# Two of the three top-16 decodes of the last routing pair, cut into steps and put beside the first expert blocks

## The chip, the cores and the metric

The kernel runs on one core of a Trainium2 chip. The metric is the device time of one execution in microseconds (us); lower is better. The time of the kernel before is the median of 3 runs.

## What is computed

One layer of a bidirectional encoder over 1024 tokens of width 1024, in 8 tiles of 128 tokens: an input projection, two kinds of attention, an output projection, a LayerNorm, and then a product-key expert layer (PEER), which is where the change lies:

```python
def peer(x, w_q, sub_keys, u, v):
    ...
    q = (xf @ w_q).reshape(n, PEER_HEADS, 2, PEER_QDIM // 2)
    sc = jnp.einsum('nhpc,hpkc->nhpk', q, sub_keys).astype(jnp.float32)
    s_top, i_top = lax.top_k(sc, PEER_TOPK)
    cand = (s_top[:, :, 0, :, None] + s_top[:, :, 1, None, :]).reshape(n, PEER_HEADS, PEER_TOPK * PEER_TOPK)
    ...
    fs, fpos = lax.top_k(cand, PEER_TOPK)
    eidx = jnp.take_along_axis(cand_idx, fpos, axis=-1)
    g = jax.nn.softmax(fs, axis=-1)
    ...
        h = jnp.einsum('cd,chkd->chk', xc, u[ec])
        a = (jax.nn.gelu(h.astype(jnp.float32), approximate=False) * gc).astype(xc.dtype)
        return jnp.einsum('chk,chkd->cd', a, v[ec])
```

For each token and each of 8 heads, two lists of 16 best keys of 128 are formed, their best 16 sums are picked (16 of 16,384 experts), and the token's output is the gated sum over its 128 experts. The layer ends in a second LayerNorm.

## The kernel before

The first 1107 us do projection, attention and routing, two tiles at a time; `route(pr)` treats tiles 2pr and 2pr+1. Per tile, routing makes 16 lists of the best 16 keys (`top16`: tiles `stop` for the values, `itop` for the indices), and `decode` (L176 to L235) turns these into 128 expert indices `eidx` and 128 gates: candidate sums `cv`, a second `top16` over them for each head, and then two sweeps of 16 small products into `big`, each closed by two reductions over `big` (L206, L221), all on VectorE (DVE), with one Exp on ScalarE (ACT).

The experts are then applied in two ways. Tiles 0 to 4 ("dense", ND = 5) go through all 16,384 experts in 128 blocks of 128 (`hstage`, `vres`, `vflush`, called from the loop at L771): per block two weight tiles of 512 KB are loaded, split into a high and a low part (ACT makes `uh`, `vh`; DVE makes `ul`, `vl`, both L86 and L87), the matmuls `h` follow (L91 to L93, 48 of 320 columns), Gelu on ACT, a product with the gates `gt` on DVE, and 30 matmuls of 512 columns for the output (`po`, `fl`). Their gates come from dense tables: those of tiles 0 and 1 are scattered into `gs` by 256 indirect DMAs of GpSimd (POOL, L165), those of tiles 2 to 4 are built in SBUF (`build`, L582) and written to `gd`. Tiles 5 to 7 ("gathered") take their 128 experts one by one: POOL gathers one row of `uv` (u and v beside each other) per token (L656, 1 MB each, four buffers), DVE makes the dot product with the token (L658), ACT its Gelu, DVE the product with the gate (L663) and adds the scaled v row to `acc` (L668; the first of a tile is L666). These are 3 x 128 = 384 gathers; `gather_gen` yields after each, and the block loop asks for as many as its line 778 says, about three a block.

The order of the work on each engine is not the order of the code. A scheduler that estimates times lays out each engine's queue when the kernel is built, from the data dependences, the room in the pools and the order of the code as priority. On the chip each engine then takes its own queue strictly in that order.

The decode's temporary tiles lie in the pool `rs`, on the right side of SBUF. When routing ends (`late.close()`, L628), the gather's pools (`x1p`, `gp`, `ga`) take that room, so that what goes there waits for the last instruction that used `rs`. The LayerNorm constants `lnt` (2 x 1024 numbers per partition) are loaded once for the first LayerNorm and again by `load_ln(1)` (L637) for the second, which first happens for tile 5, late in the expert blocks.

Of the kernel before, what the change touches and what calls it, by code (L numbers as in the profile page):

```python
# [11 lines left out]
F32 = mybir.dt.float32  # L12
# [9 lines left out]
P = 128  # L22
# [35 lines left out]
def trunk(ctx, tc, x, xt, wqk, wo, gn, sink, biasa, biasb, ln, wq, keyst, uv, ut, vt, out):  # L58
# [114 lines left out]
            new.append(st.ins)  # L173
        added[t, h] = new

    def decode(idx, g, sv, iv, pool, t=None):  # L176
        s2 = sv.rearrange("p (h two) k -> p h two k", two=2)
        fi = pool.tile([P, 8, 2, TOPK], F32, name="fi", bufs=1)
        nc.vector.tensor_copy(fi, iv.rearrange("p (h two) k -> p h two k", two=2))
# [8 lines left out]
        pos = pool.tile([P, 8, TOPK], U32, name="pos", bufs=1)  # L188
        for h in range(8):
            top16(fs[:, h, :], pos[:, h, :], cv[:, h, :], pool, NCAND)  # L190
        pf = pool.tile([P, 8, TOPK], F32, name="pf", bufs=1)
        nc.vector.tensor_copy(pf, pos)
        dlt = pool.tile([P, 8, TOPK - 1], F32, name="dlt", bufs=1)
# [8 lines left out]
        for a in range(1, TOPK):  # L202
            nc.vector.scalar_tensor_tensor(big[:, a % 8, :, :], pf, START[a] - 0.5,
                                           dlt[:, :, a - 1:a].to_broadcast([P, 8, TOPK]), op0=OP.is_ge, op1=OP.mult)
            if a % 8 == 7:
                nc.vector.tensor_reduce(ef if a == 7 else e2, bsum, AX.X, OP.add)  # L206
        nc.vector.tensor_add(ef, ef, e2)
# [8 lines left out]
        for b in range(TOPK):  # L216
            nc.vector.scalar_tensor_tensor(big[:, b % 8, :, :], pf, float(b),
                                           fi[:, :, 1, b:b + 1].to_broadcast([P, 8, TOPK]),
                                           op0=OP.is_equal, op1=OP.mult)
            if b % 8 == 7:  # L220
                nc.vector.tensor_reduce(ef if b == 7 else e2, bsum, AX.X, OP.add)  # L221
        nc.vector.tensor_add(ef, ef, e2)
# [11 lines left out]
        nc.vector.reciprocal(gs, gs)  # L234
        nc.vector.tensor_mul(gv, gv, gs[:, :, None].to_broadcast([P, 8, TOPK]))  # L235


    late = ExitStack()

    with ExitStack() as att:  # L240
# [278 lines left out]
        def route(pr):  # L519
# [14 lines left out]
                    nc.scalar.dma_start(xd[1, :, :, t * P:(t + 1) * P], f(tl[:, :, tok]))  # L534
            stop_ = {t: rs.tile([P, 16, TOPK], F32, name="stop", bufs=4) for t in tiles}
            itop = {t: rs.tile([P, 16, TOPK], U32, name="itop", bufs=4) for t in tiles}
            for c in range(16):
                if pr == 0 and c % 4 == 0:
                    raw = r1.tile([P, P, GC], F32, name="stage").rearrange("p a c -> p (a c)")
                    raw = raw.rearrange("p (n k c) -> p n k c", n=4, k=KT)  # L540
                    nc.sync.dma_start(raw, wq[c:c + 4].rearrange("n p k c -> p n (k c)"))
                kt = rw.tile([P, P], F32, name="kt")
                nc.sync.dma_start(kt, keyst[:, c, :])
                hi = rw.tile([P, KT, P], F32R, name="qhi")
                lo = rw.tile([P, KT, P], F32R, name="qlo")
                if pr == 0:
                    split(hi, lo, raw[:, c % 4])
                    nc.gpsimd.dma_start(wqd[c, 0], f(hi))
                    nc.gpsimd.dma_start(wqd[c, 1], f(lo))
                else:  # L550
                    nc.sync.dma_start(f(hi), wqd[c, 0])
                    nc.sync.dma_start(f(lo), wqd[c, 1])
                ps = ps_q.tile([P, 4, P], F32, name="pq").rearrange("p a b -> p (a b)")[:, :2 * P]
                for k in range(KT):
                    nc.tensor.matmul(ps, hi[:, k, :], th[:, k, :], start=(k == 0), stop=False)
                    nc.tensor.matmul(ps, hi[:, k, :], tl[:, k, :], start=False, stop=False)
                    nc.tensor.matmul(ps, lo[:, k, :], th[:, k, :], start=False, stop=(k == KT - 1))
                q = rw.tile([P, 2 * P], F32, name="q")
                nc.scalar.copy(q, ps)
                pc = ps_q.tile([P, 4, P], F32, name="pq")  # L560
                for n in range(2):
                    nc.tensor.matmul(pc[:, n, :], q[:, n * P:(n + 1) * P], kt, start=True, stop=True)
                sc = rw.tile([P, 2, P], F32, name="sc")
                nc.scalar.copy(sc, pc[:, 0:2, :])
                for n, t in enumerate(tiles):
                    top16(stop_[t][:, c, :], itop[t][:, c, :], sc[:, n, :], rs, P)
            dense = []
            for t in tiles:
                if t >= ND:
                    decode(eidx[t], gate[t], stop_[t], itop[t], rs)  # L570
                    continue
                idx = rs.tile([P, P], I32, name="idxd", bufs=4)
                g = rs.tile([P, P], F32, name="gated", bufs=4)
                decode(idx, g, stop_[t], itop[t], rs, t if t < NS else None)
                (dense if t < NS else todo).append((t, idx, g))
# [58 lines left out]
    nc.sync.dma_start(f(dl), xd[1])  # L634
    x1p = ctx.enter_context(tc.tile_pool(name="x1p", bufs=2, side="right"))
    x1 = {}
    load_ln(1)  # L637
    gp = ctx.enter_context(tc.tile_pool(name="gp", bufs=GBUF, side="right"))
    ga = ctx.enter_context(tc.tile_pool(name="ga", bufs=1, side="right"))
    sm = ctx.enter_context(tc.tile_pool(name="sm", bufs=2))  # L640
# [37 lines left out]
    def pump(n):  # L678
        while n > 0 and done[0] < total:
            next(gen)  # L680
            done[0] += 1
            n -= 1

    dn = ctx.enter_context(tc.tile_pool(name="dn", bufs=2))
    ph = ctx.enter_context(tc.tile_pool(name="ph", bufs=1, space=PSUM))
    RES = 3
# [84 lines left out]
    for e in range(ne):  # L771
# [3 lines left out]
        if pend is not None:  # L775
            vflush(*pend)
        pend = (e, a)
        while fed < min(total, total * (e + 4) // ne):
            pump(1)
            fed += 1  # L780
    vres(*pend)
# [81 lines left out]
```

## Time and profile before

| | us |
|---|---|
| median of 3 runs (2978.54 to 2978.84) | 2978.63 |
| the profiled execution, device time | 2985.32 |
| its span from first to last instruction | 2981.6 |
| TensorE (PE) busy | 2733.9 |
| DVE busy | 2408.1 |
| ACT busy | 1202.3 |
| POOL busy | 1065.1 |

A row of the timeline gives start, duration, engine, line, operation and operands, and in brackets the idle time of the engine before it and what ended it. A row of the windows view gives for a stretch of time the busy time and the number of instructions of PE, PE's weight loads, DVE, ACT and POOL, then the clock that PE was granted (1.00 is 2.4 GHz, 0.50 is 1.2 GHz), the share of DMA engines busy and GB/s. All times are us from the start of the span. Durations overlap their successor's start by some hundredths of a us, so what an operation costs on a full queue is the distance of two starts.

### The profile page before, as it was taken

How to read it: one execution, taken by the hardware profiler on the slowest of the kernel's cores; microseconds unless marked ns; L12 is line 12 of the kernel's file. 1: busy time of each engine (PE TensorE's matmuls, PEld its weight loads, DVE VectorE, ACT ScalarE, POOL GpSimd, SP SyncE). 2: the span in 40 equal slices, each digit the busy share in tenths (PEclk: the TensorE clock that was granted, in tenths of full speed). 3: DMA queues.
4: the chain of work that ended last, by engine and by line, in shares of the span. 5: the costliest groups of instructions: out<-in, count | busy, mean ns of one | idle time of the engine just before them, and what ended most of it. 6: DMA issues, size and time to landing. Idle time of an engine off the chain costs nothing.

```text
span 2981.6 us, 43327 instructions
## 1 busy us (share of the span) xinstructions
PE 2733.9 (92%) x15569; PEld 2357.3 (79%) x15569; DVE 2408.1 (81%) x5427; ACT 1202.3 (40%) x2486; POOL 1065.1 (36%) x732
## 2 busy tenths in 40 slices
PE   6887899897997867999999999999999999999996
PEld 4776577575785766888998899898888898988885
DVE  2344267887979988898998989999989999998965
ACT  2343154342786762333333343333333333333332
POOL 1111001078888881333333323333333333333300
PEclk8998989898997988999999999999999999999998
DMA  7688598897977767988998989998998898998851
GB/s 233 200 271 269 177 322 296 260 262 180 267 223 221 220 161 265 348 331 324 353 331 332 332 329 335 336 347 334 330 344 327 321 353 322 342 349 332 329 210 46
DMA packets 384886, 854.37 MB, mean 287 GB/s; under 512 B 83616, under 2 KB 243360, under 8 KB 333728
## 3 DMA queue, kind: packets, MB, share of 16 engines
q0 software_dynamic: 124224, 433.43, 41.3%
q1 hardware_dynamic: 230816, 388.82, 38.5%
q10 hardware_dynamic: 29632, 29.37, 3.1%
q8 instruction: 122, 2.00, 0.3%
q14 instruction: 92, 0.75, 0.1%
HBM read 765.21 MB, written 86.11 MB: 286 GB/s over the span
## 4 chain that ended last, share of the span: by engine, by line
PE 48%; DVE 5%; DMA 4%; issue 3%; ACT 2%; POOL 1%; SPq 0%; ACTq 0%; POOLq 0%; DVEq 0%
PE h L91 9%; PE h L92 8%; PE h L93 8%; PE po L736 5%; PE po L737 5%; PE po L738 5%; PE fl L737 3%; PE fl L736 3%; PE fl L738 3%; DMA uv<-in_uv_dram,eidx 2%; DMA raw<-in_ut_dram 2%; DVE uv L658 1%; DVE acc L668 1%; POOL uv L656 1%; DVE vl L87 1%
## 5 line engine op out<-in xcount | busy, mean ns | idle before, releaser
L656 POOL DMA_INDIRECT uv<-in_uv_dram,eidx x384 | 570.4, 1486 | 1162.5 <-DVE acc L668 688.5
L91 PE MATMUL h<-dh,uh 128*128 128x320 f32 x2048 | 641.3, 313 | 49.0 <-ACT uh L86 25.6
L93 PE MATMUL h<-dh,ul 128*128 128x320 f32 x2048 | 634.6, 310 | 0.8 <-DVE ul L87 0.8
L92 PE MATMUL h<-dl,uh 128*128 128x320 f32 x2048 | 634.1, 310 | 0.0
L658 DVE SCALAR_TENSOR_TENSOR uv<-uv,xg 128x1024 f32<-128x1024 f32 x384 | 467.4, 1218 | 43.1 <-DMA uv<-in_uv_dram,eidx 37.3
L165 POOL DMA_INDIRECT gs<-gated,idxd x256 | 434.9, 1699 | 171.3 <-DMA qlo<-wqd 87.0
L668 DVE SCALAR_TENSOR_TENSOR acc<-uv,hh,acc 128x1024 f32<-128x1024 f32 x381 | 487.6, 1280 | 4.3
L91 PEld LDWEIGHTS h<-dh,uh 128*128 128x128 f32 x2048 | 385.7, 188 | 83.7 <-ACT gl L718 48.6
L92 PEld LDWEIGHTS h<-dl,uh 128*128 128x128 f32 x2048 | 385.9, 188 | 10.9
L93 PEld LDWEIGHTS h<-dh,ul 128*128 128x128 f32 x2048 | 385.7, 188 | 4.9 <-DVE ul L87 1.5
L736 PE MATMUL po<-vh,ah 128*128 128x512 f32 x768 | 288.2, 391 | 1.5 <-ACT ah L86 1.5
L737 PE MATMUL po<-vl,ah 128*128 128x512 f32 x768 | 287.8, 391 | 0.0
L662 ACT ACTIVATE hh<-hh 128x1 f32<-128x1 f32 x384 | 77.6, 202 | 476.3 <-DVE uv L658 474.9
L738 PE MATMUL po<-vh,al 128*128 128x512 f32 x768 | 260.8, 391 | 0.0
L764 ACT COPY fl<-fl 128x512 f32<-128x512 f32 x252 | 147.1, 584 | 278.7 <-PE fl L738 278.5
L765 DVE TENSOR_TENSOR facc<-facc,fl 128x512 f32<-128x512 f32 x252 | 172.6, 685 | 72.8 <-ACT fl L764 72.6
L718 ACT ACTIVATE gl<-h 128x320 f32<-128x320 f32 x256 | 111.4, 435 | 254.5 <-PE h L93 244.4
L736 PE MATMUL fl<-vh,ah 128*128 128x512 f32 x512 | 201.8, 394 | 3.0 <-ACT fl L764 3.0
L737 PE MATMUL fl<-vl,ah 128*128 128x512 f32 x512 | 201.9, 394 | 0.0
L738 PE MATMUL fl<-vh,al 128*128 128x512 f32 x512 | 199.6, 390 | 0.0
L87 DVE TENSOR_TENSOR ul<-raw,uh 128x1024 fp32r<-128x1024 f32 x128 | 156.1, 1220 | 52.6 <-ACT uh L86 51.7
L86 ACT CAST uh<-raw 128x1024 fp32r<-128x1024 f32 x128 | 134.2, 1049 | 116.8 <-DMA raw<-in_ut_dram 60.7
(201 smaller groups left out, 5389.2 us busy)
## 6 DMA issues: line engine op xcount, KB each, us to landing
raw<-in_ut_dram SPq DMA_DIRECT2D x128, 512.0 KB
raw<-in_vt_dram SPq DMA_DIRECT2D x128, 512.0 KB
qhi<-wqd SPq DMA_DIRECT2D x48, 512.0 KB
qlo<-wqd SPq DMA_DIRECT2D x48, 512.0 KB
gd<-stage SPq DMA_DIRECT2D x12, 2048.0 KB
gt<-gd SPq DMA_DIRECT2D x32, 768.0 KB
wraw<-in_wqk_dram SPq DMA_DIRECT2D x36, 512.0 KB
bt<-in_biasb_dram SPq DMA_DIRECT2D x64, 288.0 KB
```

Of the source, the lines that this page charges most:

```text
L87: nc.vector.tensor_sub(lo, raw, f(hi))
L91: nc.tensor.matmul(ps, wh, mh, start=first, stop=False)
L92: nc.tensor.matmul(ps, wh, ml, start=False, stop=False)
L93: nc.tensor.matmul(ps, wl, mh, start=False, stop=last)
L165: st = nc.gpsimd.indirect_dma_start(out=gs, out_offset=bass.IndirectOffsetOnAxis(ap=idx[:, k:k + 1], axis=0), in_=g[:, k:k + 1], in_offset ...
L656: nc.gpsimd.indirect_dma_start(out=u, out_offset=None, in_=uv, in_offset=bass.IndirectOffsetOnAxis(ap=eidx[t][:, k:k + 1], axis=0))
L658: nc.vector.scalar_tensor_tensor(u[:, 0:D], u[:, 0:D], 1.0, x1[t], op0=OP.mult, op1=OP.mult, accum_out=hh[:, k:k + 1])
L668: nc.vector.scalar_tensor_tensor(acc, u[:, D:], hh[:, k:k + 1], acc, op0=OP.mult, op1=OP.add)
L736: nc.tensor.matmul(ps, ah[:, cs], vh[:, js], start=first, stop=False)
L737: nc.tensor.matmul(ps, ah[:, cs], vl[:, js], start=False, stop=False)
L738: nc.tensor.matmul(ps, al[:, cs], vh[:, js], start=False, stop=last)
L765: nc.vector.tensor_add(acc[:, j, :], acc[:, j, :], fl)
```

## The change

The decode of tiles 6 and 7, the last two, leaves `route(3)`. `decode` becomes a generator (`decode_steps`) that stops after each head's `top16` and after every fourth product, 16 times per tile; the other tiles run it to its end at once as before. For tiles 6 and 7 the lists `stop` and `itop` are written into the room of `lnt` instead of the pool `rs`, the decode's temporaries lie in the same room and in a new tile `side` (4.5 KB per partition, in the pool `dx` of the expert stage), and the block loop advances the generator two steps per block, 16 blocks in all, after which `load_ln(1)` is called. The pace at which the blocks ask for gathers changes with it: two a block for the first 18 blocks, then about 3.2.

```diff
-    def decode(idx, g, sv, iv, pool, t=None):
+    def decode(*args):
+        for _ in decode_steps(*args):
+            pass
+
+    def decode_steps(idx, g, sv, iv, pool, t=None):
...
             top16(fs[:, h, :], pos[:, h, :], cv[:, h, :], pool, NCAND)
+            yield
...
+            if a % 4 == 3:
+                yield
...
+            if b % 4 == 3:
+                yield
...
+    held = {}
+    lflat = lnt.rearrange("p a d -> p (a d)")
...
+            self.at = dict(fi=(lflat, 1024), fs=(lflat, 1280), pf=(lflat, 1408), dlt=(lflat, 1536), of=(lflat, 1536),
+                           pos=(lflat, 1792), ei=(lflat, 1792), e2=(lflat, 1920), cv=(side, 0), t16=(side, 512),
+                           big=(side, 0), ef=(side, 1024), gs=(side, 0))
...
+            if pr == 3:
+                for n, t in enumerate(tiles):
+                    stop_[t] = carve(lflat, 512 * n, [P, 16, TOPK])
+                    itop[t] = carve(lflat, 512 * n + 256, [P, 16, TOPK], U32)
+                    held[t] = stop_[t], itop[t]
...
             for t in tiles:
+                if t in held:
+                    continue
...
-    load_ln(1)
...
+    side = dx.tile([P, 9 * P], F32, name="side")
+
+    def held_decodes():
+        for t in sorted(held):
+            yield from decode_steps(eidx[t], gate[t], *held[t], Carve(side))
+
+    hd = held_decodes()
...
-        while fed < min(total, total * (e + 4) // ne):
+        for _ in range(2 if hd is not None else 0):
+            if next(hd, 0) == 0:
+                hd = None
+                load_ln(1)
+                break
+        while fed < min(total, 2 * e + 4 if e < 18 else 40 + (total - 40) * (e - 17) // (ne - 21)):
```

What the scheduler made of it, on the two engines on which the expert blocks' first matmuls depend. In these rows `gate_105`, `gate_106` and `gate_107` belong to tiles 5, 6 and 7, `eidx_103` to tile 6, and x2 at the end is a repeat count.

DVE before, from the end of tile 6's decode to the first weight splits of the blocks (the first row with `ul` is block 0's weight split):

```order
L224 TENSOR_TENSOR eidx_103<-ef,of 128x128
L195 SCALAR_TENSOR_TENSOR dlt<-dlt,wrow 128x120
L87 TENSOR_TENSOR ul<-raw,uh 128x1024
L203 SCALAR_TENSOR_TENSOR big<-pf,dlt 128x128 x7
L87 TENSOR_TENSOR vl<-raw,vh 128x1024
L87 TENSOR_TENSOR ul<-raw,uh 128x1024
L206 TENSOR_REDUCE ef<-big 128x128
L87 TENSOR_TENSOR vl<-raw,vh 128x1024
```

DVE now, first where the first gathered row is used, in the middle of tile 6's decode, whose temporaries are `lnt` and `side`:

```order
L239 TENSOR_TENSOR gate_106<-lnt 128x128
L197 CAST lnt<-lnt 128x128
L208 SCALAR_TENSOR_TENSOR side<-lnt 128x128 x7
L213 TENSOR_REDUCE side<-side 128x128
L208 SCALAR_TENSOR_TENSOR side<-lnt 128x128 x8
L695 SCALAR_TENSOR_TENSOR uv,hh<-uv,xg 128x1024
L213 TENSOR_REDUCE lnt<-side 128x128
L700 TENSOR_TENSOR hh<-hh,gate_105 128x1
```

and then, with 78 instructions between that first `uv,hh` row and it, where block 0's `ul` stands:

```order
L187 TENSOR_TENSOR side<-lnt 128x8x16
L705 SCALAR_TENSOR_TENSOR acc<-uv,hh,acc 128x1024
L124 MAX lnt<-side 128x8 x8
L125 MAX_INDEX lnt<-lnt,side 128x8
L126 MATCH_REPLACE side<-lnt,side 128x50
L125 MAX_INDEX lnt<-lnt,side 128x8 x7
L127 MAX lnt<-side 128x8
L128 MAX_INDEX lnt<-lnt,side 128x8
L126 MATCH_REPLACE side<-lnt,side 128x50
L127 MAX lnt<-side 128x8
L128 MAX_INDEX lnt<-lnt,side 128x8
L87 TENSOR_TENSOR ul<-raw,uh 128x1024
```

Before, the first gathered row is used behind the `ul` of block 3; now five `uv,hh` rows, the whole second half of tile 6's decode and the beginning of tile 7's stand ahead of the first `ul`. Tile 7's decode ends (its `eidx`) between the `ul` of blocks 5 and 6.

ACT before, from the last Exp of the decode to the first Gelu of block 0:

```order
L231 ACTIVATE gate_106<-gate_106 128x128
L616 COPY stage<-pr 128x4x128
L231 ACTIVATE gate_107<-gate_107 128x128
L86 CAST uh<-raw 128x1024
L86 CAST vh<-raw 128x1024
L86 CAST uh<-raw 128x1024
L86 CAST vh<-raw 128x1024
L718 ACT_TABLE_LOAD
L718 ACTIVATE gl<-h 128x320
```

ACT now, the same place:

```order
L240 ACTIVATE gate_106<-gate_106 128x128
L699 ACT_TABLE_LOAD
L699 ACTIVATE hh<-hh 128x1 x5
L83 DMA lnt<-in_ln_dram 128x1024
L86 CAST uh<-raw 128x1024
L86 CAST vh<-raw 128x1024
L86 CAST uh<-raw 128x1024
L699 ACTIVATE hh<-hh 128x1
L762 ACTIVATE gl<-h 128x320
```

The Gelus of the first five gathered rows and one load of `lnt` now stand ahead of block 0's `uh`; the Exp of tile 7 stands behind block 0's Gelus, between two table loads.

## Rows read from the trace of the kernel before

**Rows 1.** Busy time by engine, of the whole span.
```profile
PE 2733.9 (92%) x15569; PEld 2357.3 (79%) x15569; DVE 2408.1 (81%) x5427; ACT 1202.3 (40%) x2486; POOL 1065.1 (36%) x732
```

**Rows 2.** Windows: gap ahead of the expert blocks, their start, their long middle.
```profile
1107.70:1133.30 25.60, 0.00 (x0) 0.00 (x0) 22.31 (x116) 2.76 (x6) 7.82 (x5) 0.52 0.83 244
1133.30:1160.00 26.70, 22.84 (x119) 20.82 (x120) 24.94 (x52) 9.25 (x12) 0.90 (x1) 0.88 0.39 129
1160.00:2900.00 1740.00, 1719.56 (x9570) 1549.31 (x9569) 1574.22 (x2292) 622.89 (x1246) 569.53 (x384) 1.00 0.90 332
```

**Rows 3.** Timeline of PE: last matmuls of routing, first of block 0.
```profile
1106.33 1.36 PE L615 MATMUL pr<-pi,qj 128*128 128x128 f32 x8 [0.63 <-ACT qj L611]
1133.34 0.64 PE L91 MATMUL h<-dh,uh 128*128 128x320 f32 x1 [25.65 <-ACT uh L86]
...
1134.60 0.64 PE L93 MATMUL h<-dh,ul 128*128 128x320 f32 x1 [0.36 <-DVE ul L87]
```

**Rows 4.** Timelines of ACT and SP's DMA queue: block 0's weights.
```profile
1132.25 1.04 ACT L86 CAST uh<-raw 128x1024 fp32r<-128x1024 f32 x1 [7.02 <-DMA raw<-in_ut_dram]
...
1119.07 0.37 SPq L700 DMA_DIRECT2D gt<-gs  x1
...
1124.24 2.64 SPq L709 DMA_DIRECT2D raw<-in_ut_dram  x1
```

**Rows 5.** Waits of SP's queue, 1080 to 1200 us (total, times, longest).
```profile
SPq L700 <- DMA gs<-gated,idxd: 9.1, 2, 8.5
```

**Rows 6.** Timeline of POOL: last scatter, first gather.
```profile
1114.59 2.15 POOL L165 DMA_INDIRECT gs<-gated,idxd  x1 [0.30 <-issue]
1159.10 1.02 POOL L656 DMA_INDIRECT uv<-in_uv_dram,eidx  x1 [42.36 <-DVE eidx L224]
```

**Rows 7.** Timeline of DVE: last product of the table build, then the decode.
```profile
1104.73 0.68 DVE L606 TENSOR_TENSOR qj<-iota,tt 128x512 f32<-128x512 f32 x1
...
1110.29 1.85 DVE L206 TENSOR_REDUCE ef<-big 128x128 f32<-128x1024 f32 x1
1112.06 0.19 DVE L234 RECIPROCAL gs<-gs 128x8 f32<-128x8 f32 x1
...
1113.08 0.07 DVE L125 MATCH_VALUE_LOAD pos<-fs,cv 128x8 f32 x1
...
1113.26 0.07 DVE L125 MATCH_VALUE_LOAD pos<-fs,cv 128x8 f32 x1
...
1113.44 1.68 DVE L203 SCALAR_TENSOR_TENSOR big<-pf,dlt 128x128 f32<-128x128 f32 x8
1115.04 0.28 DVE L235 TENSOR_TENSOR gate<-gate,gs 128x128 f32<-128x128 f32 x1
1115.25 0.08 DVE L128 MATCH_VALUE_LOAD pos<-fs,t 128x8 f32 x1
```

**Rows 8.** Timeline of DVE: block 0's split, end of the decode, first gathered rows.
```profile
1133.32 1.23 DVE L87 TENSOR_TENSOR ul<-raw,uh 128x1024 fp32r<-128x1024 f32 x1 [3.31 <-ACT uh L86]
1134.47 1.49 DVE L203 SCALAR_TENSOR_TENSOR big<-pf,dlt 128x128 f32<-128x128 f32 x7
...
1157.95 0.29 DVE L224 TENSOR_TENSOR eidx<-ef,of 128x128 int32<-128x128 f32 x1
1159.60 0.82 DVE L722 TENSOR_TENSOR gl<-gl,gt 128x640 f32<-128x640 f32 x1 [1.36 <-ACT gl L718]
...
1168.13 1.23 DVE L658 SCALAR_TENSOR_TENSOR uv<-uv,xg 128x1024 f32<-128x1024 f32 x1 [5.59 <-issue]
...
1172.78 1.28 DVE L668 SCALAR_TENSOR_TENSOR acc<-uv,hh,acc 128x1024 f32<-128x1024 f32 x1
1173.98 1.22 DVE L658 SCALAR_TENSOR_TENSOR uv<-uv,xg 128x1024 f32<-128x1024 f32 x1
1175.12 0.08 DVE L658 DVE_READ_ACCUMULATOR uv<-uv,xg 128x1 f32 x1
```

**Rows 9.** Timeline of ACT: the table load ahead of the first Gelu.
```profile
1139.08 1.28 ACT L718 ACT_TABLE_LOAD   x1
```

More of the change, by code (lines that the diff above doesn't have):

```diff
@@ L235, in decode, with carve, __init__, tile @@
         nc.vector.tensor_mul(gv, gv, gs[:, :, None].to_broadcast([P, 8, TOPK]))
+    held = {}
+    lflat = lnt.rearrange("p a d -> p (a d)")
+    def carve(flat, at, shape, dt=F32):
+        n = int(np.prod(shape[1:]))
+        ap = flat[:, at:at + n]
+        if dt is not F32:
+            ap = ap.bitcast(dt)
+        names = "abcd"[:len(shape) - 1]
+        return ap.rearrange(f"p ({' '.join(names)}) -> p {' '.join(names)}", **dict(zip(names, shape[1:])))
+    class Carve:
+        def __init__(self, side):
+            self.at = dict(fi=(lflat, 1024), fs=(lflat, 1280), pf=(lflat, 1408), dlt=(lflat, 1536), of=(lflat, 1536),
+                           pos=(lflat, 1792), ei=(lflat, 1792), e2=(lflat, 1920), cv=(side, 0), t16=(side, 512),
+                           big=(side, 0), ef=(side, 1024), gs=(side, 0))
+        def tile(self, shape, dt, name, bufs=1):
+            flat, n = self.at[name]
+            return carve(flat, n, shape, dt)
     late = ExitStack()
```

## The prediction, made before the changed kernel was run

> **What bounds the kernel now.** I read the busy times first: PE is busy for 92% of the span, DVE for 81% [rows 1]. That is an average over unlike stages, so the windows come next. In the long middle of the expert blocks, 1160 to 2900 us, PE is busy 1719.6 of 1740 us at full clock, DVE 1574.2 [rows 2]: there PE is the limit, and the 9570 matmuls of that row take 1740 / 9570 = 0.182 us each, so that a block of 78 (48 for `h`, 30 for the output) takes 14.2 us. What PE loses ahead of the blocks is therefore not won back in them; the place to look at is the passage from routing to the blocks. There PE stands still from 1107.7 to 1133.3 and gets its first `h` only when ACT has made `uh` [rows 3]; ACT waited for the transfer of `raw` [rows 4]; that transfer stands in SP's queue behind the loads of `gt`, which start at 1119.07 [rows 4] because they wait for the last scatters into `gs` to land [rows 5], the last of which POOL issued at 1114.59 [rows 6]. So the gap of 25.6 us is made by the scatters and the loads behind them, not by the decode: DVE does its decode inside the gap, 22.3 of 25.6 us busy [rows 2], and PE is not waiting for it. PE's first full group of matmuls starts at 1134.60, when `ul` is there [rows 3], and up to 1160 only 119 matmuls are done in 26.7 us [rows 2], 21.6 us' worth at 0.182. From 1134.6 on that is a loss of about 25.4 - 117 x 0.182 = 4 us, part of it at the low clock. This is all that the decode of tile 7, which DVE still does there [rows 8], can cost PE today.
>
> **What the change removes.** The decode's temporaries no longer lie where the gather's buffers will, so the first gather needn't wait for the last `eidx`: before, POOL stood still for 42.4 us until 1159.10 for that [rows 6]. Now the first gather is held by what also holds `gt`, the landing of the last scatters, so it starts at about 1119.1 [rows 4]. Its row was used 9.0 us after its start (1159.10 to 1168.13) [rows 6, 8]; so the first gathered row can be used at 1119.1 + 9.0 = 1128.1. Call this time T.
>
> By the Trainium skill (DMA: Bandwidth & Descriptors, section on the anatomy of one DMA) a DMA from GpSimd takes about 2.0 us and its bytes at 436 GB/s, for 1 MB an estimate of 4.4 us. The row has 9.0 us; by the page T would be 1123.5 and the result 4.6 us lower.
>
> **What it puts in the way.** DVE takes its queue strictly in order, and now the first `uv,hh` row stands in the middle of tile 6's decode and ahead of every split of the blocks' weights. DVE gets there long before T: the table build ends at 1105.3 [rows 7], and behind it stand some dozen searches at 0.18 (two starts of the pair of instructions are 1113.08 and 1113.26), a sweep of 7 products (7 x 0.20, from 8 in 1.60), a reduction (1.77) and a sweep of 8 (1.60) [rows 7], 7 us in all: 1112.5. It then waits some 15.5 us for T, where before it decoded on.
>
> From T to the end of block 0's `ul` its queue holds, each at the distance of two starts: 5 dot products at 1.22 (1.14 and the read of the accumulator at 0.08) = 6.1 [rows 8]; 5 sums into `acc` at 1.20 = 6.0 [rows 8]; 3 reductions at 1.77 = 5.3, 16 products at 0.20 = 3.2, and 50 searches and small operations at 0.18 or somewhat less, which I take as 8.0 [rows 7]; `ul` itself at 1.15 [rows 8]. The sum is 29.7 us. ACT cannot go ahead either: its `uh` of block 0 stands behind five Gelus, which wait for the five dot products, and behind the load of `lnt`, which waits for tile 7's last candidate sums; that is about T + 24, so ACT ends just before DVE needs it. `ul` is done at 1128.1 + 29.7 = 1157.8 instead of 1133.32 + 1.23 = 1134.55 [rows 8]: **PE starts 23.3 us later**. The weights are in SBUF long before, even if the gathers slow `gt` and `raw` by 10 us; at that I cost those.
>
> **The first six blocks.** I add up DVE's queue in the same way from `ul` to `ul`: that of blocks 1 to 6 is ready 3.0, 21.4, 41.1, 58.1, 72.5 and 81.5 us after block 0's, since the rest of tile 7's decode (31 products, 4 reductions and some 40 smaller ones, 20 us) and 17 more dot products lie between them. PE, which I let lose 3 us after the gap at the low clock that the windows show there [rows 2], has 96 matmuls of `h` and 21 of the output ahead of block 2's second part, and asks for that `ul` at 3 + 117 x 0.182 = 24.3, when it is there; then every 14.2: at 38.5, and `ul` is 2.6 late; at 55.3, 2.8 late; at 72.3, 0.2 late; then DVE is ahead. Together 3 + 5.6 = 8.6 us are lost, where before it was 4: **4.6 us more**. The two more table loads that ACT now has (1.28 us each [rows 9]) stand ahead of a Gelu of block 1 for which PE has output matmuls to do meanwhile; I cost them at nothing, and 2.6 us if PE has none.
>
> **What costs nothing.** The 384 gathers, their DMAs and the blocks' loads stay; in the queue of DVE 23 to 27 dot products stand in every 8 blocks from the ninth on, before and now, whatever the new pace in the code, so the middle stage keeps its rate. The decode's own instructions are the same in number and length. The load of `lnt` moves from a place long before to two places on ACT's queue; the second is behind block 3 and waited for by nothing until tile 5's LayerNorm. POOL's order doesn't change at all, and SP's first ten transfers of the blocks neither. The end of the kernel, after the last block, is the same. The work of the eight gathers that DVE has done ahead of time is of no use to PE.
>
> **The sum**: 23.3 + 4.6 = 27.9, say +28 us. The profiled execution took 2985.3 us with a span of 2981.6, 6.7 above the median of 2978.6; the difference is added to the median: 3006.6.
>
> **The bounds.** The price that this trace doesn't show is a gather beside the loads of `gt`. Its low end is the 9.0 us that I took less 1 us for the start of POOL after a wait; its high end comes from the four first gathers (4 MB) lying with 4 MB of `gt` and `raw` on the same engines: at the 332 GB/s of [rows 2] they take 25 us, so the first may be 7 us later. I stay with 9.0, since in that row, too, other loads lay beside four gathers. The Trainium skill (DMA: Bandwidth & Descriptors, section on queues, rings and completion order) says that each engine goes round its queues packet by packet; by that a gather would get its share at once, and neither run nor row here shows it. The first blocks may cost nothing beyond today's 4 us (-4.6) and the small operations be shorter by a third (some 10 us over the passage), or they cost 13 us more, if DVE waits between its operations as it did from 1158 to 1168 [rows 8] and the table loads show. So +13 to +48: 2992 to 3027.
>
> **Rivals.** (1) *DVE is the real limit of the middle stage.* Then work done ahead by DVE counts, and only its idle time matters: 15.5 us now against the 3.3 + 1.4 + 5.6 = 10.3 of before [rows 8]: +5 us, 2984, no change that a measurement can tell (0.2%, or 6 us, is what it can). Against it: DVE is busy 90.5% there, PE 98.8% [rows 2]. Chance 0.06. (2) *Faster: the early gather frees the start.* If the first row were there before DVE comes to it, the queue would flow and `ul` be done by 1134.5, when the weights arrive; then the loss of 4 us in the start goes and some 2 to 3 us of DVE's idle time with it: -7 us, 2972. It decides at T + 29.7 < 1134.6, that is, T < 1105; but POOL issued its last scatter 9 us after that [rows 6]. It needs the scheduler's order to be other than it stands, or a gather's use not to hold the queue. Chance 0.05. (3) *Slower still: the clock.* If PE, with gaps of 3 us among the first blocks, works at 1.2 GHz for half of them, as it did in the gap's surroundings (0.52 and 0.88 [rows 2]), six blocks of 14.2 us cost up to 40 us more, of which DVE's slowness hides some half: +50, 3029. Against it: in 1133 to 1160 it kept some gaps and 0.88. Chance 0.07. (4) That the change doesn't do what its words say is part of the forecast: tile 6's decode stays wholly ahead of block 0, and tile 7's ends by block 6 and not by block 16.
>
> **Chances.** The forecast has 0.82. Slower by over 0.2%: 0.82 and 0.07 = 0.89; within 0.2%: 0.06; faster: 0.05. The range leaves out rivals 1 and 2 and most of 3.
>
> **What would show it.** In the profile of the changed kernel: POOL's first gather at about 1119; DVE idle from about 1112 to 1128 ahead of the first dot product, ended by the gather; block 0's `ul` at 1157 and PE still from 1107 to about 1153; gaps of PE for `ul` in blocks 3 and 4; from about 1240 on PE at 98 to 99% as before, some 28 us behind. It is wrong if `ul` of block 0 comes before 1140, or if the middle stage runs at another rate than 14.2 us a block.

## The result, and the profile after

The changed kernel took 3030.7 us (median of 4 runs, 3028.4 to 3035.3), the kernel before 2978.6; the ratio is 1.0185, with a 95% interval of 1.017 to 1.020. The forecast was 3006.6, with a range that ended at 3027: the direction was right, the size was not. The profiled execution has a span of 3032.9 us, 51.3 above that of before.

Busy times of the changed kernel, which answer to [rows 1]. DVE, ACT and POOL work about as long as before. PE's 15,569 matmuls take 15.4 us longer, at a mean granted clock of 0.952 instead of 0.961; for the other 36 us PE stands:

```profile
PE 2749.3 (91%) x15569; PEld 2369.2 (78%) x15569; DVE 2412.0 (80%) x5427; ACT 1206.0 (40%) x2488; POOL 1065.7 (35%) x732
```

The windows of [rows 2], now (busy time and count of PE, weight loads, DVE, ACT, POOL; granted clock, DMA share, GB/s):

```profile
1107.70:1133.30 25.60, 9.85 (x48) 8.79 (x48) 14.64 (x55) 14.53 (x30) 5.18 (x5) 0.63 0.39 123
1133.30:1160.00 26.70, 0.00 (x0) 0.00 (x0) 25.69 (x77) 1.01 (x5) 5.86 (x5) 0.50 1.04 376
1160.00:2900.00 1740.00, 1699.23 (x9412) 1531.18 (x9413) 1576.52 (x2360) 619.70 (x1231) 562.82 (x375) 0.99 0.89 328
```

PE, which began the blocks at 1133.3 before, does nothing up to 1160. In the first window it does work that before was done ahead of that window: matmuls of the table build, 18 us late. The timelines of ACT, PE and DVE there show what held them; they answer to [rows 3, 7] (the bracket is the idle time before the row and what ended it):

```profile
1110.65 0.82 ACTq L687 DMA_DIRECT2D xg<-xs  x2
1111.58 1.28 ACT L649 ACTIVATE qj<-qj,tt 128x128 f32<-128x128 f32 x4 [19.84 <-issue]
...
1113.80 7.24 PE L653 MATMUL pr<-pi,qj 128*128 128x128 f32 x32 [22.46 <-ACT stage L654]
...
1115.91 0.69 DVE L640 TENSOR_TENSOR pi<-iota,tt 128x512 f32<-128x512 f32 x1 [18.73 <-PE pr L653]
```

ACT stands for 19.8 us, until it has issued the two loads `xg<-xs` (L687, `x1` of the first two gathered tiles). They now stand on ACT's queue ahead of the build's last steps, and their room is the old `rs`, in which the indices and gates of the scatters lie. The profile names no releaser, but here and in e2 and e10 below they issue 1.7 us behind the end of the last scatter on POOL, so I take it that they wait for the scatters. PE and DVE stand behind ACT. This is a wait that the prediction didn't have. SP's queue, POOL, ACT, PE and DVE further on, which answer to [rows 3, 4, 6, 8]:

```profile
1126.30 0.32 SPq L655 DMA_DIRECT2D gd<-stage  x1
1138.38 0.37 SPq L744 DMA_DIRECT2D gt<-gs  x1
...
1150.38 2.56 SPq L753 DMA_DIRECT2D raw<-in_ut_dram  x1
...
1107.36 1.54 POOL L165 DMA_INDIRECT gs<-gated,idxd  x1 [0.30 <-issue]
1125.31 1.01 POOL L693 DMA_INDIRECT uv<-in_uv_dram,eidx  x1 [16.41 <-DVE side L126]
...
1161.26 1.04 ACT L86 CAST uh<-raw 128x1024 fp32r<-128x1024 f32 x1 [5.75 <-DVE lnt L127]
...
1162.36 0.64 PE L91 MATMUL h<-dh,uh 128*128 128x320 f32 x1 [37.33 <-ACT uh L86]
...
1134.10 1.22 DVE L695 SCALAR_TENSOR_TENSOR uv<-uv,xg 128x1024 f32<-128x1024 f32 x1 [2.57 <-issue]
...
1162.34 1.23 DVE L87 TENSOR_TENSOR ul<-raw,uh 128x1024 fp32r<-128x1024 f32 x1
```

The first gather starts at 1125.3, 0.28 us behind the end of the late build's last matmuls (as in e2 and e10, which points at the build as what holds it); its row is used 8.8 us later, and `ul` of block 0 follows 28.2 us behind that.

Since the 1080 us ahead of this differ by some 10 us from one profile to the next, I measure from the last group of projection matmuls of `route(3)` (`pq` on PE): 1083.15 before, 1081.77 now. Block 0's `ul` starts 50.2 us behind it before and 80.6 now; from there to the end of the span it is 1848.3 and 1870.6 us. So -1.4 + 30.4 + 22.3 = 51.3: **30 us ahead of block 0 and 22 behind it**, where the forecast had 23.3 and 4.6.

DVE's busy time from the last `pq` to block 12's `ul` shows both (windows view: stretch, its length, busy us, count, clock, DMA share, GB/s). The kernel before:

```profile
1083.15:1288.61 205.46, 182.63 (x457) 0.91 0.78 273
```

and the changed kernel:

```profile
1081.77:1337.32 255.55, 211.38 (x501) 0.83 0.75 270
```

Two of its costliest groups in that stretch (line, operation, operands, count, busy us, mean ns, idle time before and what ended it), in the kernel before:

```profile
L658 DVE SCALAR_TENSOR_TENSOR uv<-uv,xg 128x1024 f32<-128x1024 f32 x28 | 34.1, 1217 | 5.6 <-issue 5.6
L668 DVE SCALAR_TENSOR_TENSOR acc<-uv,hh,acc 128x1024 f32<-128x1024 f32 x26 | 33.3, 1280 | 0.3
```

and in the changed kernel, with the table build's:

```profile
L695 DVE SCALAR_TENSOR_TENSOR uv<-uv,xg 128x1024 f32<-128x1024 f32 x40 | 48.8, 1219 | 11.9 <-DMA uv<-in_uv_dram,eidx 9.2 <-issue 2.6
L705 DVE SCALAR_TENSOR_TENSOR acc<-uv,hh,acc 128x1024 f32<-128x1024 f32 x37 | 47.4, 1280 | 0.1
L640 DVE TENSOR_TENSOR pi<-iota,tt 128x512 f32<-128x512 f32 x9 | 6.2, 689 | 19.3 <-PE pr L653 19.2
```

DVE is busy for 89% of this stretch before, 183 of 205 us. Now the stretch is 50.1 us longer: DVE stands 44.2 instead of 22.8 us (+21.3; ahead of the table build's `pi` alone it stands 19.2 for the late `pr`), and it does 12 dot products and 11 sums of the gathers more ahead of block 12 (+28.8). The same work is then missing later, where PE is the limit and it buys nothing: from block 12's `ul` to block 127's it is 1630.6 us before and 1633.3 now.

### The profile page after: what moved, and what is told of

Same layout as the page of the kernel before. It is cut to its first block, busy times and chain, and to the rows that moved or that the text cites. A ratio compares the mean times of both kernels' runs of the same rounds, so it can differ in the third digit from the quotient of the medians.

```text
span 3032.9 us, 43325 instructions
## 1 busy us (share of the span) xinstructions
PE 2749.3 (91%) x15569; PEld 2369.2 (78%) x15569; DVE 2412.0 (80%) x5427; ACT 1206.0 (40%) x2488; POOL 1065.7 (35%) x732
## 4 chain that ended last, share of the span: by engine, by line
PE 47%; issue 5%; DMA 5%; DVE 4%; ACT 2%; POOL 1%; SPq 0%; ACTq 0%; POOLq 0%; DVEq 0%
PE h L91 8%; PE h L92 8%; PE h L93 8%; PE po L780 5%; PE po L781 5%; PE po L782 5%; PE fl L781 3%; PE fl L780 3%; PE fl L782 3%; DMA uv<-in_uv_dram,eidx 2%; DMA raw<-in_ut_dram 2%; POOL uv L693 1%; DVE uv L695 1%; DVE acc L705 1%; ACT uh L86 0%
## 5 line engine op out<-in xcount | busy, mean ns | idle before, releaser
L92 PEld LDWEIGHTS h<-dl,uh 128*128 128x128 f32 x2048 | 387.6, 189 | 11.2
```

Of the source, the lines that this page charges most:

```text
L92: nc.tensor.matmul(ps, wh, ml, start=False, stop=False)
```

## The experiments

Theory **A**: the stall of ACT in the table build is the loss. **B**, the prediction's: DVE's order, dot products ahead of block 0's `ul`, with the rest covered. **C**: most of the loss lies behind `ul`. After the first four runs, **D**: all that goes ahead of its turn because `rs` is free early (`x1` loads, gathers, dot products); **F**: the decode beside the blocks costs by itself. After ten, **H**: from the last `pq` to block 12 the time is DVE's, and every us in which DVE stands or does gathers is paid.

All runs (H's columns from the profiles: us from the last `pq` to the `ul` of blocks 0 and 12, DVE not busy in that stretch, dot products in it; "against before" is the median less that of the kernel before in the same group of runs; a profile is one execution, up to 7 us off the median, which is so in before, e8 and e9):

| kernel | median us | against before | ratio, 95% | `ul` 0 | `ul` 12 | DVE idle | dots |
|---|---|---|---|---|---|---|---|
| before | 2978.6 | | | 50.2 | 205.5 | 22.8 | 28 |
| changed | 3030.7 | +52.1 | 1.017 to 1.020 | 80.6 | 255.5 | 44.2 | 40 |
| e1 | 3031.7 | +52.1 | 1.014 to 1.020 | 84.3 | 250.2 | 39.7 | 40 |
| e2 | 3019.0 | +39.4 | 1.010 to 1.015 | 83.9 | 247.2 | 51.4 | 33 |
| e3 | 3003.5 | +23.9 | 1.005 to 1.010 | 67.9 | 228.1 | 32.3 | 33 |
| e5 | 2973.9 | -5.7 | 0.9965 to 0.9999 | 39.0 | 199.6 | 20.3 | 27 |
| e7 | 2989.8 | +9.9 | 1.002 to 1.006 | 50.8 | 222.6 | 28.2 | 32 |
| e8 | 2998.4 | +18.5 | 1.003 to 1.007 | 38.2 | 224.2 | 30.5 | 33 |
| e9 | 3015.6 | +35.7 | 1.008 to 1.016 | 74.2 | 235.1 | 24.8 | 39 |
| e10 | 3038.4 | +58.5 | 1.016 to 1.024 | 86.3 | 255.5 | 46.3 | 39 |
| e12 | 2982.2 | +6.0 | 1.001 to 1.004 | 50.1 | 212.5 | 25.2 | 28 |
| e11 | 2989.3 | +13.0 | 1.003 to 1.006 | 38.2 | 215.7 | 27.7 | 29 |
| e13 | 2976.0 | -2.4 | 0.997 to 1.001 | 39.3 | 195.7 | 33.2 | 20 |
| e14 | 2967.6 | -10.8 | 0.994 to 0.997 | 37.9 | 204.4 | 37.3 | 20 |

### e1: the x1 loads on POOL

```diff
-            nc.scalar.dma_start(x1[t], xs[t])
+            nc.gpsimd.dma_start(x1[t], xs[t])
```

> Only the queue of the two x1 loads (L687) changes, from ACT to POOL; DVE's and SP's orders stay as in the changed kernel. Theory A (the loads on ACT's queue held the last steps of the table build by 19.8 us, and this comes ahead of everything on DVE): the build ends again near 1105 us instead of 1122.8, the first gathered row is usable at about 1120 to 1123 instead of 1134.1, block 0's ul follows 29.5 us behind it at 1150 to 1152 instead of 1162.3, and the time falls by 10 to 13 us, to 3018 to 3021 us. Rival B (only DVE's order matters, the stall on ACT has cover): ul stays within 3 us of 1162 and the time within 3 us of 3030.7.

Measured: no change, +52.1. The build does end early again (the last `gd` store issues 25.7 us after the last `pq`, 26.0 before), but the first dot product is at 56.1 us after it, where the changed kernel has 52.3. POOL's timeline and then DVE's:

```profile
1112.49 1.54 POOL L165 DMA_INDIRECT gs<-gated,idxd  x1 [0.30 <-issue]
1116.50 1.19 POOL L687 DMA_DIRECT2D xg<-xs  x2 [2.47 <-issue]
1123.37 1.00 POOL L693 DMA_INDIRECT uv<-in_uv_dram,eidx  x1 [5.67 <-DMA gt<-gd]
...
1133.38 1.23 DVE L695 SCALAR_TENSOR_TENSOR uv<-uv,xg 128x1024 f32<-128x1024 f32 x1 [25.72 <-DMA gt<-gd]
```

On POOL the loads stand ahead of the first gather, and DVE, free of the build, stands 25.7 us at the dot product instead. Theory A had the stall right and its worth wrong: with the stall gone the first gathered row still isn't used earlier, but 3.8 us later. B's number came true, but not for its reason.

### e2: dot products behind block 0's ul

An order edge on DVE from block 0's `ul` (kept in `uls`) to the dot products; the `x1` loads stay on ACT.

```diff
+                    tc.add_manual_dep(dot.ins, uls[0].ins.name, ...NoSync..., reason="behind the block")
```

> The dot products of the gathered rows stand behind block 0's ul on DVE; the x1 loads stay on ACT. Theory A: the stall on ACT holds the last table store to 1126 us and with it the loads of gt and raw, so uh still comes near 1161 and ul near 1162; only the first blocks behind it get lighter, by 0 to 8 us: 3022 to 3031 us. Rival B (DVE's order is the whole loss at block 0): ul returns to about 1139 us and the time falls by some 23 us, to 3005 to 3010 us.

Measured: 3019.0. As A says, `ul` doesn't move (83.9; it waits for `uh`, whose `raw` stands behind the late table build), so at block 0 the stall alone is as bad as the stall with the dot products. But 11.7 us go, more than A allowed, and all behind `ul`: from there to the end it is 1853.5 us instead of 1870.6.

### e3: both

The edits of e1 and e2 together.

> Both edits: x1 loads on POOL, dot products behind block 0's ul. Theory A: table build ends near 1105, the last table store lands near 1119, raw is issued near 1124, and ul comes at 1133 to 1138, as in the kernel before; the time is 2985 to 2998 us, the rest over 2978.6 being the decode of tile 7, the table loads and the early gathers among the first twelve blocks. Rival C (the larger part of the loss lies behind ul, in the first twelve blocks, whatever comes ahead): 3003 us or more with ul at 1138 or earlier.

Measured: 3003.5, C's number, but with `ul` at 67.9, late, which C didn't have. DVE was ready (it stood 11.2 us for `uh`); what came late was the weights, as the timelines of SP's queue and ACT show:

```profile
1120.71 13.84 SPq L753 DMA_DIRECT2D raw<-in_ut_dram  x1
...
1141.51 1.04 ACT L86 CAST uh<-raw 128x1024 fp32r<-128x1024 f32 x1 [13.38 <-DMA raw<-in_vt_dram]
```

`raw` took 13.8 us to issue, where [rows 4] has 2.64; POOL had issued four gathers of 1 MB from 1120.8 on. Taking the stall away with DVE's order mended (e2 to e3) is worth 15.5 us.

### e5: the kernel before, raw of block 0 ahead of gt

```diff
+    raw0 = dn.tile(...); nc.sync.dma_start(raw0, ut[0]); load_g(0)
```

> The kernel before, with block 0's load of raw issued ahead of the four loads of gt on SP. If the landing of the last table store (issued 1109.1, its room free 1119.1) sets when raw may start, and the gt loads ahead of it the rest, raw is issued at 1119 instead of 1124.2, ul comes 5 us earlier at about 1128, and the time falls by 3 to 5 us, to 2973.5 to 2975.5 us. If the decode on DVE or the landing of gt sets the start of the blocks as well, the time stays within 1.5 us of 2978.6.

Measured: 2973.9, as expected in size. `ul` comes even 11 us earlier: in this profile the first load starts 6.6 us after the last store's issue, not 10. About half of it is lost again by block 12 (-5.9).

### e7: e3, and the first gathers behind block 0's ul

```diff
+                    if t == ND and k < 4: tc.add_manual_dep(gd_.ins, uls[0].ins.name, SYNC, reason="behind the block")
```

> As e3_both, and the first gathers on POOL also wait for block 0's ul. In e3 raw of block 0 took 13.8 us to issue on SP beside four gathers of 1 MB and uh waited for it until 1141.5. Theory D (what is left in e3 is the traffic of the early gathers ahead of raw, and dot products among the first blocks): ul comes 50 to 54 us after the last projection matmul pq of route(3), as in the kernel before (50.2), instead of 67.9 in e3, and the time falls to 2982 to 2990 us. Rival E (raw is slow to issue for another reason, such as the x1 loads on POOL's queue): ul stays at 65 us or more behind pq and the time within 4 us of 3003.5.

Measured: `ul` at 50.8, as D says, and 2989.8, the upper end of D's range. SP's queue, with no gather beside it, and ACT:

```profile
1119.66 2.64 SPq L753 DMA_DIRECT2D raw<-in_ut_dram  x1
...
1127.96 1.04 ACT L86 CAST uh<-raw 128x1024 fp32r<-128x1024 f32 x1 [23.97 <-DMA raw<-in_vt_dram]
```

So what held `raw` in e3 was the gathers beside it; keeping them back is worth 14 of the 24 us that e3 loses.

### e8: e7 with raw ahead of gt

The edits of e7 and e5 together.

> As e7, with block 0's raw loaded ahead of the gt loads as in e5. Theory D: ul comes 37 to 42 us after the last pq (39.0 in e5), and the time is 2970 to 2982 us: the steps of the decode beside the blocks cost next to nothing once the gathers stand behind. Rival F (the decode of tiles 6 and 7, now on DVE behind ul, is paid for in the first twelve blocks): ul at 37 to 42 us behind pq, but 2985 us or more.

Measured: 2998.4, a miss for D, with the `ul` that D forecast (38.2). The gathers started at 1129.4, 7 us behind this early `ul`, and ran into the next load, as ACT shows:

```profile
1121.24 1.04 ACT L86 CAST uh<-raw 128x1024 fp32r<-128x1024 f32 x1 [11.52 <-DMA gs<-gated,idxd]
...
1141.35 1.04 ACT L86 CAST vh<-raw 128x1024 fp32r<-128x1024 f32 x1 [12.66 <-DMA raw<-in_vt_dram]
```

F's number was right; this run can't tell whether its reason was.

### e9: x1 loads on ACT, behind the table build

```diff
-            nc.scalar.dma_start(x1[t], xs[t])
+            xl = nc.scalar.dma_start(x1[t], xs[t]); tc.add_manual_dep(xl.ins, late_[0][-1].ins.name, ...NoSync..., reason="behind the build")
```

`late_[0][-1]` is the last copy of `stage` in the build. DVE keeps dot products ahead of `ul`.

> The changed kernel with the x1 loads still on ACT, but behind the last copy of the table build. DVE keeps its order with dot products ahead of ul. If DVE's place for the first dot product decides (theory D), the first gather starts 2 to 5 us behind the last scatter, the first dot product 9 us later, and ul 28 to 29.5 us behind that, 68 to 78 us after the last pq (80.6 in the changed kernel, 84.3 in e1); the time is 3018 to 3028 us. If the stall on ACT was the larger part (theory A), the time is 3013 us or less, with the build's end and ul both 18 us earlier.

Measured: 3015.6, 15 us below the changed kernel, and 2.4 us under D's range. POOL and DVE:

```profile
1107.11 1.01 POOL L693 DMA_INDIRECT uv<-in_uv_dram,eidx  x1 [4.55 <-issue]
...
1117.13 1.23 DVE L695 SCALAR_TENSOR_TENSOR uv<-uv,xg 128x1024 f32<-128x1024 f32 x1 [13.18 <-DMA uv<-in_uv_dram,eidx]
```

The first row is used 43.5 us after the last `pq` and `ul` comes at 74.2. This is the kernel that the prediction described: its T, 1128.1, was 45.0 after the last `pq`, DVE was to stand 15.5 us for it (13.2), and `ul` was to start some 73.4 behind `pq`. That the sums agree is in part luck: T is 1.5 us earlier and the queue behind it 2 us longer. It is still 35.7 us slower than before, with DVE idle 2.0 us more than before (24.8 against 22.8) and busy 27.7 us more: the other cost shows in the gathers' groups up to block 12's `ul`, 39 dot products for 28:

```profile
L695 DVE SCALAR_TENSOR_TENSOR uv<-uv,xg 128x1024 f32<-128x1024 f32 x39 | 47.4, 1217 | 15.7 <-DMA uv<-in_uv_dram,eidx 15.7
```

### e10: no steps

```diff
-    hd = held_decodes()
+    for _ in held_decodes(): pass
+    hd = None; load_ln(1)
```

> The changed kernel with the two decodes written at once ahead of the first block instead of in two steps a block; lists and temporaries stay in the LayerNorm constants' room. If the steps are what costs (rival G), it returns to within 8 us of 2979. If the room is (rs free early, so x1 loads and gathers go ahead: theories A and D alike), nothing changes: within 6 us of 3030.7, ul 78 to 84 us after the last pq.

Measured: 3038.4, 1.7 us above the bound, with `ul` at 86.3, 2.3 above it. The small steps are not what costs; what is left is that the temporaries left `rs`. 39 dot products stand ahead of block 12's `ul`, 40 in the changed kernel.

### e12: gathers behind block 3's ul

```diff
-        while fed < min(total, ...
+        while e >= 3 and fed < min(total, ...
```

As e7, with `uls[3]` for `uls[0]` on the gathers, which are also written from block 3 on: about where the kernel before starts them. The decode beside the blocks is then left of the change, with the gathers' new pace and the `x1` loads on POOL.

> As e7, with the gathers on POOL and the dot products on DVE behind block 3's ul instead of block 0's, about where the kernel before has its first gather (1159.1 against block 3's ul at 1160.5). What is left of the change is the decode beside the blocks alone. Theory D (all of the loss is gathers, dot products and x1 loads going ahead): ul 50 to 52 us after the last pq, first twelve blocks at the pace of the kernel before, and 2976 to 2983 us. Rival F (the decode of tile 7 on DVE and its two table loads cost among the blocks what is left in e7, some 10 us): 2986 to 2993 us.

Measured: 2982.2, in D's range; 6.0 us above before. DVE's dot products up to block 12's `ul`:

```profile
L695 DVE SCALAR_TENSOR_TENSOR uv<-uv,xg 128x1024 f32<-128x1024 f32 x28 | 34.1, 1218 | 3.4 <-DMA uv<-in_uv_dram,eidx 3.4
```

As many dot products as before (28), and block 12 comes 7.0 us later: DVE is busy 187.2 us in it (182.6 before) and stands 25.2 (22.8). So 46 of the change's 52 us go when `x1` loads, gathers and dot products stand back.

### e11: e12 with raw ahead of gt

The edits of e12 and e5 together.

> As e12, with block 0's raw loaded ahead of the gt loads. In e8 the gathers began at once behind an early ul, and block 0's vh waited 12.7 us for its raw load beside them; here they begin behind block 3. Theory D: ul 37 to 42 us after the last pq, vh within 10 us of uh, no such wait, and 2966 to 2976 us, below the kernel before. Rival F: 2980 us or more.

Measured: 2989.3, a miss for D and inside F's range: `ul` is 12 us earlier than in e12, and the end is 7 later. Block 4's `ul` is at 102.7, in e12 at 106.8: two thirds of the start were given back within four blocks. This led to H: with TensorE started early, DVE still has decode and gathers to do ahead of block 12, and that sum, not the start, is the limit.

But traffic isn't excluded. Block 0's `vh` waited only 4.1 us for its load; block 4's waited 10.6, and DVE and PE stood behind it. Its load stands behind a pair of `gt` loads, among gathers, with the DMA engines at a share of 1.03 from 1180 to 1197. SP's queue, ACT, DVE and PE:

```profile
1180.49 2.11 SPq L771 DMA_DIRECT2D raw<-in_vt_dram  x1
...
1196.92 1.04 ACT L86 CAST vh<-raw 128x1024 fp32r<-128x1024 f32 x1 [10.61 <-DMA raw<-in_vt_dram]
...
1198.00 1.22 DVE L87 TENSOR_TENSOR vl<-raw,vh 128x1024 fp32r<-128x1024 f32 x1 [8.46 <-ACT vh L86]
...
1202.37 0.64 PE L91 MATMUL h<-dh,uh 128*128 128x320 f32 x1 [7.52 <-ACT gl L762]
```

This one wait of PE, 7.5 us, is as long as what e11 lies above e12, which has none like it. H as the reason for e11 is therefore argued and not shown.

### e13 and e14: gathers behind block 6's ul, raw first

e13 is the kernel before with e5's edit and the gathers written from block 6 on, behind `uls[6]`; e14 is e11 with 6 for 3.

> The kernel before, block 0's raw ahead of the gt loads (as e5) and the first gathers behind block 6's ul. Theory H (from the last pq to block 12's ul the time is DVE's: idle time plus decode plus block work plus the gathers' dot products and accumulations, 67 us of them before; work of theirs that is put later runs in slack): the gathers' work in that stretch falls from 63 to about 45 us, block 12's ul comes less than 199.6 us after the last pq (e5), as far as TensorE allows, and the time is 2963 to 2973 us. Rival I (TensorE bounds these blocks already, and gathers put later come back at the end): 2973 to 2980 us.

> As e11, with the gathers behind block 6's ul instead of block 3's. Theory H: the gathers' work on DVE ahead of block 12's ul falls from 69 to about 45 us, which pays for the decode there; block 12's ul comes some 15 to 20 us earlier than in e11 (215.7 after the last pq), and the time falls from 2989 to 2968 to 2978 us. Rival F (the decode beside the blocks costs by something else, its table loads or its waits): 2984 us or more.

Measured: e13 takes 2976.0 us, in rival I's range and above H's. It has as few dot products as e14 and block 12's `ul` at 195.7, earlier than e5, as H says. But that buys nothing in the time: against before e13 is at -2.4, e5 at -5.7, and e13's runs lie between 2963 and 2990 us.

e14 takes 2967.6 us, below every other kernel here, ratio 0.9942 to 0.9974, at the low end of H's range. Against e11 only the gathers' start differs, and 24 us go (+13.0 to -10.8). The gathers' groups on DVE up to block 12's `ul` in e11:

```profile
L695 DVE SCALAR_TENSOR_TENSOR uv<-uv,xg 128x1024 f32<-128x1024 f32 x29 | 35.3, 1216 | 2.2 <-DMA uv<-in_uv_dram,eidx 2.2
L705 DVE SCALAR_TENSOR_TENSOR acc<-uv,hh,acc 128x1024 f32<-128x1024 f32 x27 | 34.5, 1279 | 0.2
```

and in e14:

```profile
L695 DVE SCALAR_TENSOR_TENSOR uv<-uv,xg 128x1024 f32<-128x1024 f32 x20 | 24.4, 1226 | 7.2 <-DMA uv<-in_uv_dram,eidx 7.2
L705 DVE SCALAR_TENSOR_TENSOR acc<-uv,hh,acc 128x1024 f32<-128x1024 f32 x18 | 23.1, 1283 | 0.1
```

Nine dot products and nine sums fewer are 22.3 us of DVE, near the 24 us, but that doesn't show the cause. In the two profiles the stretch to block 12's `ul` is shorter by 11.3 us, where H had 15 to 20, because DVE now stands 37.3 us in it. From there to the end of the span another 14.4 us go (1678.4 for 1692.8), in a part where H has no gain, and no run here says why. And 7.5 of the 11.3 can be the wait for block 4's load, shown under e11: e14 has no gather in flight at that place. So H and the traffic aren't told apart in this pair, and what makes e14 the fastest stays open.

F's number is out: the kernel with the decode beside the blocks is no slower than before once the gathers stand back to block 6. Whether that decode is itself a gain isn't settled: e14 lies 8 us below e13, but the two intervals meet.

## Why the prediction was wrong in size

1. **What bounds the kernel: half right.** PE is the limit of the middle, and there the changed kernel runs at the old rate. That "the place to look at is the passage from routing to the blocks" held. But the passage was taken to end with block 0 and a few gaps. The lag grows from 30 us at block 0's `ul` to 50 at block 12's and then stays between 46 and 53. Neither of the two signs of being wrong that were named (`ul` of block 0 before 1140, another rate in the middle) came; neither looks at the blocks between.
2. **The first gather is early and its first dot product stands ahead of block 0: right.** From T to the end of `ul` the queue was forecast at 29.7 us and took 29.5 (1134.10 to 1163.57). The 9.0 us from a gather's start to its use were 8.8 here and 10.0 in e1 and e9. The estimate of 4.4 us by the Trainium skill (DMA: Bandwidth & Descriptors, section on the anatomy of one DMA) was reached in none of these three, each of which had four gathers and other loads side by side.
3. **T: failed, by 7 us.** T was to be 45.0 us after the last `pq`; it was 52.3. The step that failed is in "what costs nothing" and in "the table build ends at 1105.3": of the moved instructions' DMAs, the two `x1` loads were not followed onto ACT's queue, ahead of the last products and copies of the build, where they held it up for 19.8 us. With the loads behind the build (e9) T was 43.5 and `ul` at 74.2, within 1 us of the forecast of 73.4; that edit gains 15 us in the median. e1 adds that it is T that counts, not which engine stands: with the loads on POOL, DVE's 25.7 us at the dot product replaced its 18.7 in the build. Nor were the weights "in SBUF long before": with the build late, `raw` of block 0 was issued only at 1150.4. The Trainium skill says (DMA: Bandwidth & Descriptors, section on the anatomy of one DMA) that a DMA's semaphore wait happens on the issuing engine's sequencer; ACT's 19.8 us agree. By the Trainium skill (the same page, section on issuing engines not being separate DMA queues), starting transfers on several engines saves only the time to start them; here the choice of the engine also decided what stood behind the wait.
4. **The first blocks at +4.6: the larger failure.** From block 0's `ul` to the end the loss was 22.3. The distances of the next six `ul` were forecast at 3.0, 21.4, 41.1, 58.1, 72.5 and 81.5; they came at 8.8, 28.4, 47.8, 66.1, 82.3 and 93.2, so the sums were short by 6 to 12, and the loss was counted only until "DVE is ahead". DVE got no further ahead: 40 dot products instead of 28 lie before block 12. What shows the price best is e2, where only DVE's order was edited: with block 0's `ul` as late as in the changed kernel, it has seven dot products and seven sums fewer before block 12 (17.9 us of DVE) and is 17 us shorter from `ul` on (11.7 in the median). On PE the loss is 21 us of waiting between the `ul` of blocks 0 and 12 instead of 5, of which 14.1 are for Gelus on ACT; ACT in turn waits 54.8 us in this stretch for gathered rows' dot products on DVE, 35.7 before. So the loss reaches PE by way of ACT. Whether the sum of DVE's work decides or the place of the gathered rows in the queues isn't told apart: e2 changes both.
5. **"The work that DVE has done ahead is of no use to PE": right, and too mild.** In the changed kernel it costs its length as long as DVE sets the pace (e2, e9) and ACT behind it; in e13 putting it off bought nothing. The text had rival 1 (DVE as the limit) only for the middle stage and only as a reason for a smaller loss.
6. **Table loads at nothing: right.** PE's waits for Gelu (`gl`) in the twelve blocks did grow; from the view of waits (us in total, times, longest), the changed kernel first, then the kernel before:

```profile
PE h L91 <- ACT gl L762: 14.1, 8, 6.0
```

```profile
PE h L91 <- ACT gl L718: 4.3, 5, 1.6
```

   But the longest, 6.0, ends before the two loads. It ends with a Gelu of block 0 that stands on ACT behind casts waiting for `raw` and behind a gathered row's Gelu waiting for its dot product. PE and then ACT:

```profile
1174.84 0.63 PE L91 MATMUL h<-dh,uh 128*128 128x320 f32 x1 [6.02 <-ACT gl L762]
...
1174.25 0.20 ACT L699 ACTIVATE hh<-hh 128x1 f32<-128x1 f32 x1 [3.17 <-DVE uv L695]
1174.36 0.42 ACT L762 ACTIVATE gl<-h 128x320 f32<-128x320 f32 x1
...
1182.80 1.28 ACT L240 ACT_TABLE_LOAD   x1
...
1184.42 1.28 ACT L762 ACT_TABLE_LOAD   x1
```

   From 1181 to 1192 PE has no gap: it does output matmuls meanwhile, as the prediction said. In e11 and e14, where the Exp waits over 4 us for DVE between the loads, PE stands 2.5 us behind them. e12 has both loads too, and its whole loss is 6.0.
7. **The bounds.** The high end let a gather be 7 us later for the traffic of four gathers beside `gt` and `raw`. The traffic was real, but its victim was the other one, `raw`: 13.8 us to issue in e3. In the changed kernel block 0 doesn't show it: there ACT's `uh` waits for DVE, not for `raw`.
8. **Rivals.** The clock (3) gave 3029, near the result, but that is luck: it supposed half of the first six blocks at 1.2 GHz. From block 0's `ul` to block 12's the granted clock is 0.94, before 0.98, and 809 matmuls take 0.190 us each instead of 0.180: some 8 us by these rows, an estimate, of the 22. e2 has nearly the same clock there, 0.95, and is 11.6 us shorter, so that part isn't the clock's. Faster (2) needed T before 1105; T was 1134. That the steps don't do what the words say (4) is borne out by e10: without steps, the same loss.

## What to carry to other kernels

A change that frees a pool's room early lets everything that waited for the room go ahead, loads as well as work, and each lands on some engine's in-order queue: follow each of them, queue by queue, to what stands behind it. Where an engine is nearly full over a stretch (DVE was busy 183 of 205 us here), add up its work to the end of that stretch as well as its waits: work pulled in from a later, slacker stretch can be paid in full (e2, e9). Putting such work off is no sure gain: moving the gathers from block 3 to block 6 was worth 24 us with the decode beside the blocks (e11 to e14), for reasons that aren't separated, and nothing in the kernel before (e5 to e13). An early start of the next stage can be given back behind it, half of it by block 12 in e5 and all of it in e11.

## What the runs showed of the hardware that was not expected

- How long an issue on SP's queue took differed with what else moved. The load of block 0's `raw` took 2.64 us to issue in the kernel before and in e7, 4.32 in e1 and 13.84 in e3; in the last two POOL started four gathers of 1 MB in the same microseconds. The second load `gt<-gs`, 2.31 before, took 9.13 in the changed kernel.
- A gather behind a plain load on POOL started late: 5.67 us after the `xg` loads in e1, 5.65 in e3, 5.84 in e8, with another releaser named each time (a `gt` load, two different DVE instructions). What POOL does in that time isn't shown.
- Gathers beside the loads of `gt` and `raw` kept the DMA engines at a share of 1.04 and 376 GB/s from 1133 to 1160 in the changed kernel, more than the 332 GB/s of the long middle [rows 2].
